# Sliding-window heads of a hybrid attention block: the softmax division moved to ScalarE, the low words of q placed by DMA, and the small softmax operations done once per head

## The chip, the core and the metric

One core of one Trainium2 chip runs the whole kernel as a single launch. The time is device microseconds (us) of that core, from the launch's start to its end; lower is better. The kernel before takes 830.82 us, the median of three runs (830.65 to 831.07).

## The reference

The block normalises x (512 tokens, 2048 channels), multiplies it by one wide input matrix, runs two groups of attention heads, gates each group with SiLU, multiplies by an output matrix, adds x and normalises again. The change lies in the second group alone: sixteen heads of 64 channels, two key/value heads, a window of 128 tokens and a learned sink per head.

```python
def _masked_softmax(s, mask, sink=None):
    s = jnp.where(mask, s.astype(jnp.float32), NEG_INF)
    m = jnp.maximum(jnp.max(s, axis=-1, keepdims=True), sink)
    e = jnp.where(mask, jnp.exp(s - m), 0.0)
    denom = jnp.sum(e, axis=-1, keepdims=True) + jnp.exp(sink - m)
    return e / jnp.maximum(denom, TINY)
...
qb = _rope(_heads(qb, N_HEADS_B, HEAD_DIM_B)).reshape(B, S, N_KV_B, GROUP_B, HEAD_DIM_B)
o_b = _banded_attention(qb, _rope(kb), vb, WIN_B, sink=sinks)   # blocks of 128 queries x 256 keys
y_b = o_b.reshape(B, S, WIDTH_B) * jax.nn.silu(zb)
```

## The kernel before

All products run on TensorE in single-precision "words": a float32 operand is split into a high word (rounded to the format that TensorE takes at full rate) and a low word (the rest), and a product is three matmuls, high by high, high by low, low by high (the helper `mm3`, L112 to L115). So each operand needs a copy that makes the high word (ScalarE, e.g. L89) and a subtraction that makes the low word (VectorE, e.g. L90).

The program is written as a sequence, and a planner puts it in order: it works through the program with an estimate of each instruction's time and gives every engine one fixed order, so work that stands later in the program fills the gaps of earlier work. Buffers come from tagged pools: a tile takes one of the `bufs` buffers of its tag and holds it until its last reader is done. A pool that is opened after another one was closed lies in the memory that the closed one leaves.

The stages: the first projections and the compressed keys (up to about 180 us); the eight heads of the first group, functions `pair` and `attn_a` (to about 471 us); the second group (to about 690 us), which the change touches; the output projection and the last normalisation.

The second group handles two heads at a time, in eight rounds i = 0 to 7 ("pair i" below). The loop at L880 to L896 does for each: `softmax_b(i)`; the projection of the next pair's q, `proj(wz[17+i])`, and its evacuation `qb_evac`; the gate projection `proj(wz[24+i])` with its evacuation `z_evac`; and `attn_b(i)`. Ahead of the loop stand the projection of the keys (L876), that of q for pair 0 (`wz[16]`, L877), and `build_k`, `build_v`, which make the words of keys and values.

- `proj` (L398) sums 48 matmuls of 512 columns into one bank of the accumulator memory, a tile with tag `pj`. That tag has two buffers, so a third projection can start only when one of the two before has been read out.
- `q_rope` (L463) reads the bank with three VectorE operations (L118, L119, L120) into `t1` and `t2`, which GpSimd adds (L468). `t1` and `t2` have one buffer each, and `z_evac` (L455) takes the `t2` buffer too for its `zr` (L458).
- `qb_evac` (L785) makes two operands of 128 rows from `t1`. ScalarE copies `t1` into both (L795). Then, for each of the two heads and each half of the channels, VectorE overwrites 32 rows with the low words of the 32 rows beside them (L799, four per pair). A matmul against the stacked keys so sums high and low words at once.
- `softmax_b` (L803) works in two parts of two query blocks each. In a part: the scores on TensorE (L820, L821), one VectorE operation per block and head that scales, masks and takes the row minimum (L824), the minimum with the sink (L827), the sink's exponent (L828, L829), the exponentials with their row sums on ScalarE (L834), the addition and the reciprocal (L835, L836), and the division as a multiplication by the reciprocal on VectorE (L841). The score blocks `ttb` have six buffers, the scores' banks `spb` two.
- `attn_b` (L844) transposes the blocks on TensorE (L855), splits them (L508, L509), multiplies by the values (L861, L862, L867) and evacuates (L871, L872, L489).

The pool `wb`, which holds `vbf`, `kd`, the keys' words, `ttb` and other tiles of this group, is opened at L751, after the pools of the first group were closed (L743, L746). The pool `wk` with `t1`, `t2` and the q operands is older and lasts through both groups. Once the last gate projection is done, the memory of x is closed (L889) and `yh`, `yl`, the words of the attention's output, are made there (L909, L910) for the output projection (accumulators `oa`).

Of the kernel before, what the change touches and what calls it, by code (L numbers as in the profile page):

```python
# [10 lines left out]
F32 = mybir.dt.float32  # L11
F32R = mybir.dt.float32r
AF = mybir.ActivationFunctionType
ALU = mybir.AluOpType
# [3 lines left out]
P = 128  # L18
S = 512
D = 2048  # L20
KT = D // P
NQ = S // P
# [4 lines left out]
SCALE_B = 64 ** -0.5  # L27
# [7 lines left out]
def hybrid_block(ctx, tc, xT, xtm, w0, w1s, w2s, wz, wq, wkb, wo0, wos, cw1, cw2, cpos, rope, tabs, sinks, gT, fg, out):  # L35
    nc = tc.nc
    pe, act, dve, pool = nc.tensor, nc.scalar, nc.vector, nc.gpsimd

    def sb(name, bufs=1, side=None):
        return tc.tile_pool(name=name, bufs=bufs, side=side)  # L40
# [8 lines left out]
    bmask = tab[:, 512 + NQ * CMP:768 + NQ * CMP]  # L49
# [413 lines left out]
    def q_rope(ps, cos, sin, t1=None):  # L463
        if t1 is None:
            t1 = wk.tile([P, S], F32, name="t1", tag="t1", bufs=1)
        t2 = wk.tile([P, S], F32, name="t2", tag="t2", bufs=1)
        rope_mul(t1, t2, ps, cos, sin)
        pool.tensor_tensor(out=t1, in0=t1, in1=t2, op=ALU.add)  # L468
        return t1
# [33 lines left out]
    wk = wks.enter_context(sb("wk", bufs=2))  # L503
# [102 lines left out]
    for m in range(8):  # L606
        j, r = m // 4, m % 4
# [142 lines left out]
    pssb = psb.enter_context(tc.tile_pool(name="pssB", bufs=2, space=PSUM, side="right"))  # L750
    wb = wbs.enter_context(sb("wb"))  # L751
# [33 lines left out]
    def qb_evac(ps, i):  # L785
        t1 = q_rope(ps, cosB, sinB)
        if i % 2:
            both = wk.tile([P, 2, S], F32R, name="qs", tag="raw3", bufs=1)
            where = [both[:, v, :] for v in range(2)]
        else:  # L790
            where = [wk.tile([P, S], F32R, name="qs", tag=f"q{w}", bufs=1) for w in "hl"]
        q2 = []
        for v in range(2):
            qs = where[v]
            act.activation(qs, t1, AF.Copy)  # L795
            for half in range(2):
                r = half * 64 + v * 32
                d = half * 64 + 32 - v * 32
                dve.tensor_tensor(out=qs[d:d + 32], in0=t1[r:r + 32], in1=qs[r:r + 32].bitcast(F32), op=ALU.subtract)  # L799
            q2.append(qs)  # L800
        return q2

    def softmax_b(i, q2):  # L803
        g = i // 4
        tts = []
        skb = sk[:, 0, 2 * i:2 * i + 2].unsqueeze(1).to_broadcast([P, 2, 2])
        nskb = sk[:, 1, 2 * i:2 * i + 2].unsqueeze(1).to_broadcast([P, 2, 2])
        for part in range(2):
            mn = wk.tile([P, 2, 2], F32, name="mnb", tag="mnb")
            dn = wk.tile([P, 2, 2], F32, name="dnb", tag="dnb")  # L810
            ex = wk.tile([P, 2, 2], F32, name="exb", tag="exb")
            for e in range(2):
                qt = 2 * part + e
                tt = wb.tile([P, 2, 256], F32, name="ttb", tag="ttb", bufs=6)
                tts.append(tt)
                ko = max(qt - 1, 0) * P
                qs = slice(qt * P, (qt + 1) * P)
                sp = pssb.tile([P, 2, 256], F32, name="spb", tag="spb")
                for v in range(2):
                    pe.matmul(sp[:, v, :], q2[v][:, qs], KBH[:, g, ko:ko + 256], start=v == 0, stop=False)  # L820
                    pe.matmul(sp[:, v, :], q2[v][:, qs], KBL[:, g, ko:ko + 256], start=False, stop=v == 1)  # L821
                n = 256 if qt else 128
                for v in range(2):
                    dve.tensor_tensor_reduce(out=tt[:, v, 0:n], in0=sp[:, v, 0:n], in1=bmask[:, 256 - n:256],  # L824
                                             scale=-SCALE_B, scalar=1e38, op0=ALU.add, op1=ALU.min,
                                             accum_out=mn[:, e, v:v + 1])
            dve.tensor_tensor(out=mn, in0=mn, in1=nskb, op=ALU.min)  # L827
            dve.tensor_tensor(out=ex, in0=mn, in1=skb, op=ALU.add)  # L828
            act.activation(ex, ex, AF.Exp)  # L829
            for e in range(2):  # L830
                n = 256 if part or e else 128
                for v in range(2):
                    tv = tts[2 * part + e][:, v, 0:n]
                    act.activation(tv, tv, AF.Exp, bias=mn[:, e, v:v + 1], scale=-1.0, accum_out=dn[:, e, v:v + 1])  # L834
            dve.tensor_tensor(out=dn, in0=dn, in1=ex, op=ALU.add)  # L835
            dve.reciprocal(dn, dn)  # L836
            for e in range(2):
                n = 256 if part or e else 128
                for v in range(2):
                    tv = tts[2 * part + e][:, v, 0:n]  # L840
                    dve.tensor_scalar(tv, tv, dn[:, e, v:v + 1], None, op0=ALU.mult)  # L841
        return tts

    def attn_b(i, tts, st):  # L844
# [164 lines left out]
    for t in range(NQ):  # L1009
        v = xs0[t // 2][:, t % 2, :]  # L1010
# [308 lines left out]
```

## Time and profile before

| | us |
|---|---|
| median of three runs | 830.82 |
| the profiled execution, device time | 829.19 |
| its span, first to last instruction | 827.4 |
| TensorE busy | 811.5 (98%) |
| VectorE busy | 662.1 (80%) |
| ScalarE busy | 485.6 (59%) |
| GpSimd busy | 89.3 (11%) |

The profile is of one execution. Its engines are PE (TensorE), PEld (TensorE's weight loads, beside PE), DVE (VectorE), ACT (ScalarE), POOL (GpSimd) and SP (the queue that issues most DMAs). L12 is line 12 of the kernel. A group's row gives engine, operation, output and inputs, shape and type, count, busy time and mean, and the idle time of its engine just before it with what ended that. Rows of a timeline begin with start and length in us. Rows of windows give start and end, then the window's length, then busy time and count of each engine, the granted clock of TensorE as a share of full speed, the DMA engines' busy share and GB/s. Times inside the profile count from the start of the span.

### The profile page before, as it was taken

The page shows a single profiled execution, that of the slowest core. Times are in us where ns is not written, and L with a number is a line of the kernel's source. Part 1 is how long each engine was busy: PE and PEld are TensorE (multiplying, and loading weights), DVE is VectorE, ACT ScalarE, POOL GpSimd, SP SyncE. Part 2 cuts the span into 40 slices and gives each one's busy share as a digit, 9 for nine tenths or more (in the row PEclk, how much of TensorE's full clock was granted, in tenths as well). Part 3 has the DMA queues.
Part 4 walks back from the last instruction along what each step waited for, and adds up shares of the span by engine and source line. Part 5 has one row for each costly group of instructions (what it writes and reads, how often), then busy time and mean ns, then how long its engine had stood idle before and what let it go on. Part 6 is the DMA issues. An engine that isn't in the chain of part 4 may idle for free.

```text
span 827.4 us, 14161 instructions
## 1 busy us (share of the span) xinstructions
PE 811.5 (98%) x5278; PEld 735.6 (89%) x5278; DVE 662.1 (80%) x1311; ACT 485.6 (59%) x1026; POOL 89.3 (11%) x69
## 2 busy tenths in 40 slices
PE   9999999999999999999999999999999999999996
PEld 7788898999999999999888888888888788999996
DVE  6869786966799898999766688877677798877895
ACT  6734456564676786787665365645444647554555
POOL 3600002011001001101011121011011000110000
PEclk9999999999999999999999999999999999999998
DMA  9665885898330222522733321222222226797845
GB/s 324 194 206 166 281 290 200 265 371 284 103 111 22 99 77 92 166 90 89 251 107 102 99 92 56 74 80 74 77 76 77 77 62 241 235 251 198 244 96 203
DMA packets 52117, 128.30 MB, mean 155 GB/s; under 512 B 4945, under 2 KB 17233, under 8 KB 52049
## 3 DMA queue, kind: packets, MB, share of 16 engines
q1 hardware_dynamic: 50032, 120.59, 43.3%
q0 software_dynamic: 1728, 6.29, 4.3%
q8 instruction: 41, 0.67, 0.3%
q10 hardware_dynamic: 288, 0.52, 0.2%
q14 instruction: 28, 0.22, 0.1%
HBM read 110.31 MB, written 17.07 MB: 154 GB/s over the span
## 4 chain that ended last, share of the span: by engine, by line
PE 84%; DVE 6%; DMA 5%; issue 2%; ACT 2%; SPq 0%; DVEq 0%; ACTq 0%; POOLq 0%
PE pj L115 16%; PE pj L113 15%; PE pj L114 15%; PE bank L115 4%; PE bank L113 4%; PE oa L114 4%; PE oa L113 4%; PE oa L115 3%; PE sp L539 3%; PE bank L114 3%; PE tp L855 2%; DMA rw<-wos 1%; PE tp L577 1%; DMA xr<-xT 1%; DMA raw<-cw 1%
## 5 line engine op out<-in xcount | busy, mean ns | idle before, releaser
L115 PE MATMUL pj<-xh,wlo 128*128 128x512 f32 (+1 forms) x560 | 196.0, 350 | 2.0 <-DVE wlo L617 1.5
L113 PE MATMUL pj<-xh,whi 128*128 128x512 f32 (+1 forms) x560 | 196.2, 350 | 0.8 <-DVE t L665 0.8
L114 PE MATMUL pj<-xl,whi 128*128 128x512 f32 (+1 forms) x560 | 195.4, 349 | 0.0
L90 DVE TENSOR_TENSOR wlo<-raw,whi 128x1024 fp32r<-128x1024 f32 (+2 forms) x102 | 115.3, 1135 | 37.5 <-ACT whi L89 36.6
L89 ACT ACTIVATE whi<-raw 128x1024 fp32r<-128x1024 f32 (+1 forms) x101 | 95.2, 944 | 80.6 <-PE pj L114 24.0
L115 PEld LDWEIGHTS pj<-xh,wlo 128*128 128x128 f32 x560 | 105.3, 188 | 16.3 <-DVE wlo L617 2.2
L113 PEld LDWEIGHTS pj<-xh,whi 128*128 128x128 f32 x560 | 105.4, 188 | 14.2 <-DVE t L665 1.2
L114 PEld LDWEIGHTS pj<-xl,whi 128*128 128x128 f32 x560 | 105.3, 188 | 13.4 <-issue 0.7
L617 DVE TENSOR_TENSOR wlo<-raw,whi 128x1024 fp32r<-128x1024 f32 x49 | 61.6, 1260 | 10.3 <-ACT whi L616 9.9
L616 ACT ACTIVATE whi<-raw 128x1024 fp32r<-128x1024 f32 x49 | 51.7, 1056 | 24.7 <-PE pj L114 12.7
L113 PE MATMUL oa<-whi,yh 128*128 128x256 f32 (+1 forms) x168 | 50.1, 299 | 0.6 <-ACT yh L909 0.6
L114 PE MATMUL oa<-wlo,yh 128*128 128x256 f32 (+1 forms) x168 | 50.4, 300 | 0.2 <-DVE wlo L1147 0.2
L115 PE MATMUL oa<-whi,yl 128*128 128x256 f32 (+1 forms) x168 | 49.7, 299 | 0.0
L834 ACT ACTIVATE ttb<-ttb,mnb 128x256 f32<-128x256 f32 (+1 forms) x64 | 30.1, 471 | 26.0 <-DVE mnb L827 25.5
L509 DVE TENSOR_TENSOR pl<-tp,ph 128x512 fp32r<-128x512 f32 x56 | 37.6, 683 | 6.6 <-ACT ph L508 6.6
L508 ACT ACTIVATE ph<-tp 128x512 fp32r<-128x512 f32 x56 | 32.3, 592 | 17.9 <-PE tp L577 11.2
L114 PE MATMUL bank<-wlo,xh 128*128 128x256 f32 (+1 forms) x128 | 40.2, 316 | 0.0
L115 PE MATMUL bank<-whi,xl 128*128 128x256 f32 (+1 forms) x128 | 39.9, 314 | 0.0
L468 POOL TENSOR_TENSOR t<-t,t 128x512 f32<-128x512 f32 x9 | 19.3, 2147 | 176.4 <-DVE t L120 176.4
L113 PE MATMUL bank<-xh,whi 128*128 128x512 f32 x96 | 37.0, 396 | 1.1 <-ACT whi L89 0.7
L113 PE MATMUL bank<-whi,xh 128*128 128x256 f32 (+1 forms) x128 | 36.7, 318 | 1.3 <-ACT whi L89 1.3
L114 PE MATMUL bank<-xl,whi 128*128 128x512 f32 x96 | 37.0, 391 | 0.0
(356 smaller groups left out, 2202.2 us busy)
## 6 DMA issues: line engine op xcount, KB each, us to landing
raw<-wz SPq DMA_DIRECT2D x36, 512.0 KB, 3.6
raw<-wq SPq DMA_DIRECT2D x28, 512.0 KB, 3.7
raw<-cw SPq DMA_DIRECT2D x16, 512.0 KB, 5.0
raw<-wos SPq DMA_DIRECT2D x12, 512.0 KB, 5.0
rw<-wos SPq DMA_DIRECT2D x10, 512.0 KB, 5.5
xr<-xT SPq DMA_DIRECT2D x16, 256.0 KB, 5.0
raw<-w SPq DMA_DIRECT2D x8, 512.0 KB, 4.2
fd<-ft SPq DMA_DIRECT2D x4, 1024.0 KB, 5.9
```

Of the source, the lines that this page charges most:

```text
L89: last["hi"] = act.activation(hi[:, :width], rw[:, :width], AF.Copy).ins
L90: last["lo"] = dve.tensor_tensor(out=lo[:, :width], in0=rw[:, :width], in1=hi[:, :width].bitcast(F32), op=ALU.subtract).ins
L113: pe.matmul(ps, ah, bh, start=first, stop=False, skip_group_check=go_on)
L114: pe.matmul(ps, ah, bl, start=False, stop=False, skip_group_check=go_on)
L115: recent["mm"] = pe.matmul(ps, al, bh, start=False, stop=last, skip_group_check=go_on).ins
L468: pool.tensor_tensor(out=t1, in0=t1, in1=t2, op=ALU.add)
L508: act.activation(ph, tp, AF.Copy)
L509: dve.tensor_tensor(out=pl, in0=tp, in1=ph.bitcast(F32), op=ALU.subtract)
L539: pe.matmul(sp[:, a:b], qq[:, qs], kk[0][:, ko:ko + b - a], start=pi == 0, stop=pi == 2)
L616: act.activation(hi, src, AF.Copy)
L617: last["lo"] = dve.tensor_tensor(out=lo, in0=src, in1=hi.bitcast(F32), op=ALU.subtract).ins
L834: act.activation(tv, tv, AF.Exp, bias=mn[:, e, v:v + 1], scale=-1.0, accum_out=dn[:, e, v:v + 1])
```

## The change

In `qb_evac`, one subtraction over all 128 rows makes a tile `low` (new, in the pool `wb`, one buffer), and four DMAs on the SP queue place its quarters, 32 rows of 2 KB each, into the two q operands. In `softmax_b` the two parts become one: the small tiles hold all four query blocks, and L827, L828, L829, L835 and L836 are issued once per pair in place of twice. The division is a ScalarE copy with a scale per row in place of a VectorE multiplication. The score blocks still have six buffers. No matmul is added or taken away.

```diff
+        low = wb.tile([P, S], F32R, name="low", tag="low")
+        for qs in where:
             act.activation(qs, t1, AF.Copy)
+        dve.tensor_tensor(out=low, in0=t1, in1=where[0].bitcast(F32), op=ALU.subtract)
+        for v, qs in enumerate(where):
             for half in range(2):
                 r = half * 64 + v * 32
                 d = half * 64 + 32 - v * 32
-                dve.tensor_tensor(out=qs[d:d + 32], in0=t1[r:r + 32], in1=qs[r:r + 32].bitcast(F32), op=ALU.subtract)
+                nc.sync.dma_start(qs[d:d + 32].bitcast(F32), low[r:r + 32].bitcast(F32))
...
-        for part in range(2):
-            mn = wk.tile([P, 2, 2], F32, name="mnb", tag="mnb")
+        mn = wk.tile([P, NQ, 2], F32, name="mnb", tag="mnb")
+        for qt in range(NQ):
...
+        dve.tensor_tensor(out=mn, in0=mn, in1=nskb, op=ALU.min)
+        dve.tensor_tensor(out=ex, in0=mn, in1=skb, op=ALU.add)
+        act.activation(ex, ex, AF.Exp)
+        for qt in range(NQ):
+            for v in range(2):
+                tv = tts[qt][:, v, 0:256 if qt else 128]
+                act.activation(tv, tv, AF.Exp, bias=mn[:, qt, v:v + 1], scale=-1.0, accum_out=dn[:, qt, v:v + 1])
+        dve.tensor_tensor(out=dn, in0=dn, in1=ex, op=ALU.add)
+        dve.reciprocal(dn, dn)
...
-                    dve.tensor_scalar(tv, tv, dn[:, e, v:v + 1], None, op0=ALU.mult)
+                act.activation(tv, tv, AF.Copy, scale=dn[:, qt, v:v + 1])
```

More of the change, by code (lines that the diff above doesn't have):

```diff
@@ L791, in qb_evac @@
             where = [wk.tile([P, S], F32R, name="qs", tag=f"q{w}", bufs=1) for w in "hl"]
-        q2 = []
-        for v in range(2):
-            qs = where[v]
+        low = wb.tile([P, S], F32R, name="low", tag="low")
+        for qs in where:
             act.activation(qs, t1, AF.Copy)
+        dve.tensor_tensor(out=low, in0=t1, in1=where[0].bitcast(F32), op=ALU.subtract)
+        for v, qs in enumerate(where):
             for half in range(2):
@@ L798, in qb_evac @@
                 d = half * 64 + 32 - v * 32
-                dve.tensor_tensor(out=qs[d:d + 32], in0=t1[r:r + 32], in1=qs[r:r + 32].bitcast(F32), op=ALU.subtract)
-            q2.append(qs)
-        return q2
+                nc.sync.dma_start(qs[d:d + 32].bitcast(F32), low[r:r + 32].bitcast(F32))
+        return where
     def softmax_b(i, q2):
@@ L805, in softmax_b @@
         tts = []
-        skb = sk[:, 0, 2 * i:2 * i + 2].unsqueeze(1).to_broadcast([P, 2, 2])
-        nskb = sk[:, 1, 2 * i:2 * i + 2].unsqueeze(1).to_broadcast([P, 2, 2])
-        for part in range(2):
-            mn = wk.tile([P, 2, 2], F32, name="mnb", tag="mnb")
[L810 to L841, printed above, removed]
@@ new lines, in softmax_b @@
+        skb = sk[:, 0, 2 * i:2 * i + 2].unsqueeze(1).to_broadcast([P, NQ, 2])
+        nskb = sk[:, 1, 2 * i:2 * i + 2].unsqueeze(1).to_broadcast([P, NQ, 2])
+        mn = wk.tile([P, NQ, 2], F32, name="mnb", tag="mnb")
+        dn = wk.tile([P, NQ, 2], F32, name="dnb", tag="dnb")
+        ex = wk.tile([P, NQ, 2], F32, name="exb", tag="exb")
+        for qt in range(NQ):
+            tt = wb.tile([P, 2, 256], F32, name="ttb", tag="ttb", bufs=6)
+            n = 256 if qt else 128
+            tts.append(tt)
+            ko = max(qt - 1, 0) * P
+            qs = slice(qt * P, (qt + 1) * P)
+            sp = pssb.tile([P, 2, 256], F32, name="spb", tag="spb")
+            for v in range(2):
+                pe.matmul(sp[:, v, :], q2[v][:, qs], KBH[:, g, ko:ko + 256], start=v == 0, stop=False)
+                pe.matmul(sp[:, v, :], q2[v][:, qs], KBL[:, g, ko:ko + 256], start=False, stop=v == 1)
+            for v in range(2):
+                dve.tensor_tensor_reduce(out=tt[:, v, 0:n], in0=sp[:, v, 0:n], in1=bmask[:, 256 - n:256],
+                                         scale=-SCALE_B, scalar=1e38, op0=ALU.add, op1=ALU.min,
+                                         accum_out=mn[:, qt, v:v + 1])
@@ new lines, in softmax_b @@
+        dve.tensor_tensor(out=mn, in0=mn, in1=nskb, op=ALU.min)
+        dve.tensor_tensor(out=ex, in0=mn, in1=skb, op=ALU.add)
+        act.activation(ex, ex, AF.Exp)
+        for qt in range(NQ):
+            for v in range(2):
+                tv = tts[qt][:, v, 0:256 if qt else 128]
+                act.activation(tv, tv, AF.Exp, bias=mn[:, qt, v:v + 1], scale=-1.0, accum_out=dn[:, qt, v:v + 1])
+        dve.tensor_tensor(out=dn, in0=dn, in1=ex, op=ALU.add)
+        dve.reciprocal(dn, dn)
+        for qt in range(NQ):
+            for v in range(2):
+                tv = tts[qt][:, v, 0:256 if qt else 128]
+                act.activation(tv, tv, AF.Copy, scale=dn[:, qt, v:v + 1])
```

## The prediction

> **What bounds the kernel now.** I read the windows first, then TensorE's waits, then the timelines around the two ends of the second group. Windows (start and end, length, then busy us of PE, PEld, DVE, ACT, POOL, the granted clock, DMA share, GB/s):
>
> ```profile
> 478.00:655.00 177.00, 177.00 (x927) 148.67 (x926) 139.03 (x374) 92.17 (x232) 14.98 (x8) 1.00 0.24 76
> 657.00:700.00 43.00, 43.00 (x195) 34.83 (x196) 39.91 (x86) 26.93 (x55) 0.00 (x0) 1.00 0.39 127
> 700.00:819.00 119.00, 118.76 (x1024) 117.66 (x1023) 99.22 (x128) 64.12 (x98) 10.64 (x12) 1.00 0.74 213
> ```
>
> All waits of TensorE between 430 and 710 us (what waited, on whom, us in total, times, longest):
>
> ```profile
> PE oa L113 <- ACT yh L909: 0.6, 1, 0.6
> ```
>
> The reader is to see that TensorE has work in hand through the whole second group, 177.00 of 177.00 us, and goes on so to 819 us. VectorE is busy for 139 of those 177 us, but TensorE never waits for it. The only wait in the group is 0.6 us at its end. Busy could still be slow, so I looked at the pace: the 512-column matmuls start 0.23 us apart (468.64 and 468.87 in a fence below) at a granted clock of 1.00. The change takes away no matmul. So it can gain at most about 0.6 us here, whatever it does for VectorE, and it can lose wherever TensorE runs out of work. The question is which tile comes later than before.
>
> **The change part by part.** The sum is made against the profiled execution, 829.19 us (its span of 827.4 and 1.8 around it). That is 1.6 under the median of the three runs, 830.82; I add the difference found to the median.
>
> *Amounts.* Groups by shape, 440 to 700 us (the ScalarE rows from 330 to 700):
>
> ```profile
> L799 DVE TENSOR_TENSOR qs<-t,qs 32x512 fp32r<-32x512 f32 x32 | 21.8, 683 | 1.6 <-ACT qs L795 0.7
> L841 DVE TENSOR_SCALAR ttb<-ttb,dnb 128x256 f32<-128x256 f32 x48 | 14.4, 357 | 0.2
> L841 DVE TENSOR_SCALAR ttb<-ttb,dnb 128x128 f32<-128x128 f32 x16 | 3.8, 283 | 0.2
> L910 DVE TENSOR_TENSOR yl<-yp,yh 128x512 fp32r<-128x512 f32 x16 | 10.4, 677 | 0.2 <-ACT yh L909 0.2
> L567 ACT ACTIVATE tt<-tt,dn 128x256 f32<-128x256 f32 x8 | 3.6, 499 | 0.0
> L567 ACT ACTIVATE tt<-tt,dn 128x128 f32<-128x128 f32 x8 | 2.7, 392 | 0.0
> L834 ACT ACTIVATE ttb<-ttb,mnb 128x256 f32<-128x256 f32 x48 | 23.8, 497 | 9.5 <-DVE mnb L827 9.0
> ```
>
> VectorE loses the 32 quarter subtractions (21.8 us) and the divisions (14.4 + 3.8 = 18.2), gains eight subtractions of 128x512 at 0.68 as in L910 (5.4), and does half of its small operations: some 35 us less, and more with the small ones. ScalarE gains 48 x 0.50 + 16 x 0.39 = 30.2 us, as L567 shows for the same scaling in the first group. In the 177 us window ScalarE is busy for 92, so it has room on average. Both amounts are off TensorE's path, and I cost them at nothing in the middle of the group. The cover is the product work that TensorE has in hand.
>
> *Middle of the group.* Rounds repeat every 27.9 us. Of one round (engine timelines):
>
> ```profile
> 593.68 0.15 DVE L827 TENSOR_TENSOR mnb<-mnb,sk 128x4 f32<-128x4 f32 x1
> 596.49 1.14 DVE L841 TENSOR_SCALAR ttb<-ttb,dnb 128x256 f32<-128x256 f32 x4
> 604.47 1.15 ACT L795 ACTIVATE qs<-t 128x512 fp32r<-128x512 f32 x2 [3.38 <-POOL t L468]
> 605.14 2.79 DVE L799 TENSOR_TENSOR qs<-t,qs 32x512 fp32r<-32x512 f32 x4
> 610.65 1.03 PE L855 MATMUL tp<-ident,ttb 128*128 128x128 f32 x8
> 611.44 0.36 PE L820 MATMUL spb<-KBH,qs 128*128 128x256 f32 x1
> ```
>
> The score blocks are divided by 597.6 and transposed at 610.65: 13 us to spare. Done at once per pair, the last minimum still comes near 593.7. Then follow eight exponentials (6 x 0.50 + 2 x 0.39 = 3.8), the sums and reciprocal (0.4) and eight divisions (3.8), which ends near 602 and leaves 8. The q operands are ready at 607.9 and used at 611.44, so 3.5 to spare. In their place: first copy 605.1, `low` 605.8, four issues of 0.33 (as that of `vbf` below), and a landing. No row shows a 64 KB transfer between two tiles. The nearest are (KB each, median us from issue to landing):
>
> ```profile
> yd<-st SPq DMA_DIRECT2D x8, 256.0 KB, 2.4
> sk<-sinks SPq DMA_DIRECT2D x1, 8.0 KB, 4.5
> raw<-wz SPq DMA_DIRECT2D x36, 512.0 KB, 3.6
> ```
>
> That puts the last quarter between 609.2 and 611.3, still ahead of 611.44. I take 0, by the row that also leaves a tile of this core; the other end, behind a weight load (another 3.6), is 3.5 us in a round, and I keep half a microsecond a round, 3.5 for seven, in the range. The issues stand in SP's queue ahead of weight loads, which wait for `low` with them; these loads wait for a free buffer anyway (the queue's rows put 132 us on that, quoted below), so a microsecond costs nothing.
>
> *Start of the group.* Here I expect the loss. `low` lives in the pool `wb`; the quarter subtractions of before wrote only into `wk`. When does `wb`'s memory come free? SP's waits from 440 to 660 us, then timelines:
>
> ```profile
> SPq L85 <- DVE wlo L90: 132.4, 23, 8.6
> SPq L758 <- PE op L600: 0.2, 1, 0.2
> ...
> 446.22 2.77 DVE L799 TENSOR_TENSOR qs<-t,qs 32x512 fp32r<-32x512 f32 x4
> 449.02 0.17 DVE L556 TENSOR_SCALAR dn<-dn 128x6 f32<-128x6 f32 x1
> 454.62 0.69 DVE L118 TENSOR_TENSOR t<-pj,cosA 128x512 f32<-128x512 f32 x1 [3.41 <-PE pj L115]
> 468.84 0.69 DVE L458 TENSOR_TENSOR zr<-pj,rstdb 128x512 f32<-128x512 f32 x1 [2.56 <-PE pj L115]
> 471.49 0.69 DVE L489 SCALAR_TENSOR_TENSOR st<-op,st 128x512 f32<-128x512 f32 x1
> 471.48 0.33 SPq L758 DMA_DIRECT2D vbf<-vbd x1
> 472.10 1.70 DVE L776 COPY kd<-kb 32x512 f32<-32x512 f32 x4
> ...
> 468.64 0.39 PE L113 MATMUL pj<-xh,whi 128*128 128x512 f32 x1
> 468.87 0.39 PE L114 MATMUL pj<-xl,whi 128*128 128x512 f32 x1
> 470.84 0.61 PE L600 MATMUL op<-pd,VF 128*128 128x128 f32 x4
> ```
>
> `vbf`, the first tile of `wb`, waits for L600, the last matmul of the first group, though that matmul has nothing to do with `vbf`; so the pool as a whole seems to come free when L600 ends, at 470.84 + 0.61 = 471.45. Before, pair 0's low words were written at 446 to 449, which released `t1`, and pair 1's rotation (L118) read its bank at 454.62. With the change `low` of pair 0 waits for L600, so `t1` stays taken and pair 1's rotation waits. Its bank of `pj` stays taken too. The other bank gets the gate product of pair 0 (read out at 468.84), whose `zr` wants the buffer of `t2`, and the waiting rotation holds that if its L119 goes ahead. Then the next product has no bank. Before, it began at 468.64 (the next starts 0.23 later), and six of its matmuls stand ahead of L600's end. Without them L600 is done near 471.45 - 6 x 0.23 = 470.1, and TensorE is out of work.
>
> What it waits for then: `low` (0.68), `kd` (1.70, earlier in the program), L118 (0.69), 0.1 of signalling, 3.2 in all. VectorE's freed 2.8 us at 446 let L556 start about 0.6 earlier (it was queued behind L799), and L600 with it. I take 3.2 - 0.6 = **2.6 us**. Ends: 0 if the gate's evacuation frees a bank in time; 5.2 if L489 (0.69) and both L119 and L120 (1.4) come in the same stretch and nothing is gained earlier. Only a late operand of pair 0 could follow, but its keys' words are ready no earlier than near 474 either.
>
> *End of the group.* The last pair has no next q product to hide behind. Timelines:
>
> ```profile
> 647.33 0.60 PE L855 MATMUL tp<-ident,ttb 128*128 128x128 f32 x4
> 648.52 1.05 ACT L89 ACTIVATE whi<-raw 128x1024 fp32r<-128x1024 f32 x1
> 655.24 1.06 ACT L89 ACTIVATE whi<-raw 128x1024 fp32r<-128x1024 f32 x1
> 655.27 1.03 PE L855 MATMUL tp<-ident,ttb 128*128 128x128 f32 x8
> 656.21 4.26 ACT L909 ACTIVATE yh<-yp 128x512 fp32r<-128x512 f32 x8
> ```
>
> The third and fourth score blocks need buffers that the pair before gives back with its last transposes (647.33). Before, only the second part's four exponentials came after that; VectorE divided, TensorE transposed at 655.27, and ScalarE was free for `yh`, for which TensorE waits. After, ScalarE has eight exponentials from 649.6, behind the weight copy (3.8, to 653.4), sums (0.4), eight divisions (3.8, or 3.2 overlapped as neighbours) to about 657.2, and a weight copy of 1.06 that may stand before or between. `yh` moves from 656.2 to between 656.2 (if it is put ahead of the divisions) and 659.6; the transposes move into the gap. I take **1.2 us**, from 656.2 to the end of the divisions plus a signal, with bounds -0.6 (the wait of today gone) and 3.4. Behind it, VectorE is busy for 39.9 of 43 us and keeps its order, and I add nothing.
>
> Sum: 2.6 + 1.2 = 3.8 us; 829.2 becomes 833.0, and on the median 830.8 + 3.8 = **834.6 us**.
>
> **Rivals.** *The gate's evacuation goes first.* If the planner gives `t2`'s buffer to `zr` at 468.84, a bank is free at 469.5, before TensorE runs out at 470.1, and the start costs nothing. For it: VectorE idles 2.56 us there. Against it: L119 could run from 454.6 and takes `t2` earlier. What decides is which of the two writes that buffer first. With the end at 1.2 or less the time is 830.3 to 832.0, 831.4 by the middle: not slower by the bound below. The same time results if `low` lies in memory that is free before L600; the wait of `vbf` speaks against it. 34%.
>
> *The hold is longer and the clock drops.* At the end of the run the clock follows TensorE's idleness (last matmul ends at 819.8):
>
> ```profile
> 819.55 0.28 PE L115 MATMUL oa<-whi,ql 128*128 128x256 f32 x1
> ...
> 822.00:824.00 2.00, 0.00 (x0) 0.00 (x0) 0.60 (x1) 0.78 (x2) 0.00 (x0) 0.77 0.61 226
> 824.00:828.00 4.00, 0.00 (x0) 0.00 (x0) 0.00 (x0) 0.00 (x0) 0.00 (x0) 0.50 0.40 149
> ```
>
> A mean of 0.77 between 1.00 and 0.50 puts the drop at 823.1, 3.3 us after the last matmul. My 2.6 stays below that, the upper end 5.2 does not. How long half speed would last no row shows; if as long as the drop took, 3.3 us at half pace lose 1.7. Then 5.2 + 1.7 + 1.2 = 8.1, 838.9 us; without the drop, but with 3.5 for late quarters, 3.8 + 3.5 = 7.3, 838.1. 14%. The Trainium skill, TensorE: Matmul & The Clock Gate, section HAM oscillation, states that idle gaps over about 3.4 us bring the half clock back; by its window an estimate of the loss is 1.7 us, and the trace agrees on the drop with 3.3 us.
>
> *Relief of VectorE pays.* Gone wait at 656 and an order with fewer gaps between 700 and 819 (0.24 idle there): 0.6 + 0.24, 830.0 us, inside the bound. A gain beyond it would need matmuls closer than 0.23 us, which nothing here does. 6% for a gain by a way that I don't see, at about 828.5.
>
> **How the numbers follow.** Forecast 46% (832.6 to 836.5), first rival 34%, second 14%, relief 6%. A difference of 0.2%, 1.7 us, is about what a measurement of this kernel can tell from no change. Faster 0.06; same 0.34; slower 0.46 + 0.14 = 0.60. The range leaves out the gain and the part of the long hold above 838.5: 829.9 to 838.5.
>
> **What would show it.** Right at the start: `low` of pair 0 begins just after L600, the second L118 of the group moves from 454.6 to beyond 470, and TensorE shows a wait on VectorE of 2 to 4 us near 470. Wrong: `low` at about 446, or L458 still at 468.8 with no wait. Right at the end: `yh` near 657.5 behind L841's copies, and TensorE waits 1 us or more there. In the middle: no wait of TensorE on SP's transfers; waits at L820 would mean that the quarters land late. The forecast as a whole is wrong if TensorE's idle time is the same as before.

## The result, and the profile after

The changed kernel takes 842.52 us (median of 4 runs, 841.38 to 843.52) against 830.95 us for the kernel before (4 runs, 830.65 to 831.37): the ratio is 1.0134, 95% interval 1.0115 to 1.0152. It is some 11.6 us slower; the forecast was 3.8 slower, and 842.52 lies above the range. The profiled execution took 841.38 us, its span is 839.6 (before: 829.19 and 827.4). Lines of the changed kernel's page are a few lower than before: the q copies are L794, `low` L795, its DMAs L800, the scores L819 and L820, the division L837, the transposes L851, `yh` L905.

The windows after, with the same columns as those of before in the prediction:

```profile
478.00:655.00 177.00, 177.00 (x924) 148.29 (x923) 101.75 (x252) 105.72 (x261) 13.62 (x7) 1.00 0.27 82
657.00:700.00 43.00, 41.91 (x197) 33.52 (x196) 34.37 (x71) 27.30 (x60) 0.00 (x0) 1.00 0.29 86
700.00:819.00 119.00, 115.06 (x950) 111.91 (x950) 99.10 (x133) 63.69 (x100) 10.63 (x12) 1.00 0.74 208
```

TensorE's waits over the whole of the changed kernel, the four that touch the second group or what follows it:

```profile
PE spb L819 <- DMA qs<-low: 7.4, 1, 7.4
PE oa L114 <- DVE wlo L910: 3.5, 3, 1.7
...
PE oa L113 <- ACT yh L905: 1.1, 1, 1.1
...
PE oa L114 <- DVE wlo L1143: 0.5, 1, 0.5
```

The reader is to see that VectorE's busy time in the middle falls from 139 to 102 us and that TensorE still has work for 177.00 of 177.00: the relief is there and buys nothing. The loss stands at the seams, 7.4 us at the start of the group and 3.5 in the output projection.

**The start.** TensorE, then VectorE, then SP's queue:

```profile
467.59 0.60 PE L600 MATMUL op<-pd,VF 128*128 128x128 f32 x4
475.63 0.77 PE L819 MATMUL spb<-KBH,qs 128*128 128x256 f32 x2 [7.43 <-DMA qs<-low]
476.19 0.63 PE L113 MATMUL pj<-xh,whi 128*128 128x512 f32 x1
...
478.33 0.58 PE L115 MATMUL pj<-xh,wlo 128*128 128x512 f32 x1
478.74 0.40 PE L113 MATMUL pj<-xh,whi 128*128 128x512 f32 x1
```

```profile
467.82 1.23 DVE L90 TENSOR_TENSOR wlo<-raw,whi 128x1024 fp32r<-128x1024 f32 x1 [4.11 <-ACT whi L89]
469.08 0.69 DVE L489 SCALAR_TENSOR_TENSOR st<-op,st 128x512 f32<-128x512 f32 x1
469.69 0.68 DVE L795 TENSOR_TENSOR low<-t,qs 128x512 fp32r<-128x512 f32 x1
470.29 1.70 DVE L776 COPY kd<-kb 32x512 f32<-32x512 f32 x4
472.02 0.69 DVE L118 TENSOR_TENSOR t<-pj,cosA 128x512 f32<-128x512 f32 x1
...
473.43 0.68 DVE L120 TENSOR_TENSOR t<-pj,sinA 64x512 f32<-64x512 f32 x1
475.59 0.69 DVE L458 TENSOR_TENSOR zr<-pj,rstdb 128x512 f32<-128x512 f32 x1 [1.48 <-POOL t L468]
```

```profile
468.23 0.33 SPq L758 DMA_DIRECT2D vbf<-vbd x1
...
470.39 2.76 SPq L800 DMA_DIRECT2D qs<-low x4
```

`low` of pair 0 comes after L600, and pair 1's rotation (L118) moved from 454.62 to 472.02. L600 ends at 468.19. Until the wait's end at 475.63 stand, in order: a weight split and L489 (1.50), `low` (0.60), `kd` (1.73), L118 to L120 (2.09, to 474.11), and 1.52 until the last quarter lands. The four DMAs are issued from 470.39 on, beside `kd` and the rotation, so only their last 1.52 us add to the wait. The scores of pair 0, which read the quarters, stand in TensorE's order ahead of the third product. The first matmuls then start 0.43 us apart instead of 0.23. Windows around it, same columns:

```profile
470.00:472.00 2.00, 0.00 (x0) 0.00 (x0) 1.95 (x5) 0.73 (x2) 0.36 (x1) 0.97 0.80 178
472.00:474.00 2.00, 0.00 (x0) 0.00 (x0) 1.95 (x3) 0.63 (x1) 2.00 (x2) 0.50 0.88 314
...
476.00:478.00 2.00, 2.00 (x7) 1.61 (x7) 0.68 (x2) 1.96 (x5) 0.00 (x0) 0.50 0.39 131
478.00:480.00 2.00, 2.00 (x9) 1.62 (x8) 0.99 (x2) 1.13 (x3) 0.79 (x1) 0.82 0.14 33
```

A mean of 0.97 puts the clock's drop near 471.9, 3.7 us after the last matmul; full speed is back by 478.74. The two score matmuls took 0.56 instead of 0.24 to the next start, and the six starts from 476.19 to 478.74 took 2.55 instead of 1.38: half speed cost 1.5 us. With the wait, 8.9 us.

**The end.** ScalarE, TensorE, VectorE and SP after the last pair's scores:

```profile
661.24 0.49 ACT L831 ACTIVATE ttb<-ttb,mnb 128x256 f32<-128x256 f32 x1
...
662.68 3.22 ACT L905 ACTIVATE yh<-yp 128x512 fp32r<-128x512 f32 x6
...
666.43 2.70 ACT L905 ACTIVATE yh<-yp 128x512 fp32r<-128x512 f32 x5
669.03 3.08 ACT L837 ACTIVATE ttb<-ttb,dnb 128x128 f32<-128x128 f32 x8
...
663.35 0.50 PE L113 MATMUL oa<-whi,yh 128*128 128x512 f32 x1 [1.09 <-ACT yh L905]
...
701.78 0.69 DVE L489 SCALAR_TENSOR_TENSOR yp<-ob,st 128x512 f32<-128x512 f32 x1
702.55 0.89 SPq L1004 DMA_DIRECT2D xs<-xtm x2
```

The same two kinds of event in the kernel before, with its first output matmul:

```profile
656.87 0.50 PE L113 MATMUL oa<-whi,yh 128*128 128x512 f32 x1 [0.56 <-ACT yh L909]
...
691.41 0.69 DVE L489 SCALAR_TENSOR_TENSOR yp<-ob,st 128x512 f32<-128x512 f32 x1
692.19 0.89 SPq L1008 DMA_DIRECT2D xs<-xtm x2
```

The planner put eleven `yh` copies ahead of the last pair's eight divisions. The last pair is therefore finished (L489) 38.4 us after the first output matmul, where it was 34.5. In both kernels the first load into the last stage's new pools (`xs`) starts within 0.1 us of that L489's end: the program opens these pools after it has closed `wb` and `wk`. So the loads into them (`xs`, then `rw` and `ch`) come 3.9 us later against the work that needs them. TensorE waits 3.5 us for low words of weights (L910), in three places, and not all of them are for these loads:

```profile
715.59 1.21 DVE L910 TENSOR_TENSOR wlo<-raw,whi 128x1024 fp32r<-128x1024 f32 x1
...
716.86 0.39 PE L114 MATMUL oa<-wlo,ph 128*128 128x256 f32 x1 [1.68 <-DVE wlo L910]
...
728.71 0.39 PE L114 MATMUL oa<-wlo,yh 128*128 128x256 f32 x1 [0.79 <-DVE wlo L910]
```

The first, 1.7 us, is for words of a `raw`, a buffer from before, whose load was issued by 696.8, ahead of that L489. VectorE has had no gap since 702.38, and the planner put this split behind four additions (L1007): this wait comes from VectorE's queue and not from a late load. Only the other two, 1.8 us together, are for words of `ch`, which is loaded behind L489.

Put together from these rows, against the profile of before: the first q evacuation was 1.8 us earlier (439.13 against 440.97; the change is not in that stretch), from there to the first output matmul it takes 224.22 against 215.90, 8.3 more, and from there to the span's end 176.25 against 170.53, 5.7 more: -1.8 + 8.3 + 5.7 = 12.2, the difference of the spans. TensorE's waits tell the same without the opening: all in the list of waits come to 8.1 us before and 18.9 after, 10.8 more, and with 1.5 at half speed that is 12.3. So the -1.8 is work that the planner placed elsewhere, not a gain.

### The profile page after: what moved, and what is told of

The parts are those of the page before. It is cut to its first block, busy times and chain, and to the rows that moved or that the text cites. A ratio compares the mean times of both kernels' runs of the same rounds, so it can differ in the third digit from the quotient of the medians.

```text
span 839.6 us, 14182 instructions
## 1 busy us (share of the span) xinstructions
PE 813.3 (97%) x5278; PEld 736.5 (88%) x5278; DVE 624.4 (74%) x1191; ACT 507.0 (60%) x1082; POOL 88.2 (11%) x69
## 4 chain that ended last, share of the span: by engine, by line
PE 79%; DVE 7%; DMA 7%; ACT 3%; issue 3%; POOL 1%; SPq 0%; DVEq 0%; ACTq 0%; POOLq 0%
PE pj L115 15%; PE pj L113 15%; PE pj L114 15%; PE bank L115 4%; PE bank L113 4%; PE bank L114 3%; PE sp L539 3%; PE oa L114 3%; PE oa L113 3%; PE oa L115 3%; DMA rw<-wos 2%; PE tp L851 1%; DMA ch<-wos 1%; PE tp L577 1%; DMA xr<-xT 1%
## 5 line engine op out<-in xcount | busy, mean ns | idle before, releaser
L115 PE MATMUL bank<-whi,xl 128*128 128x256 f32 (+1 forms) x128 | 39.9, 314 | 0.0
L822 DVE CUSTOM_DVE_ANT_0 ttb<-spb,tab 128x256 f32<-128x256 f32 (+1 forms) x64 | 22.1, 386 | 21.6 <-PE spb L820 17.9
L665 DVE TENSOR_TENSOR raw<-raw 128x1024 f32<-128x1024 f32 x28 | 36.2, 1291 | 0.2
```

Of the source, the lines that this page charges most:

```text
L115: recent["mm"] = pe.matmul(ps, al, bh, start=False, stop=last, skip_group_check=go_on).ins
L665: return dve.tensor_tensor(out=out, in0=a, in1=b, op=op).ins
```

## The experiments

Four theories. A: the start's loss comes from the memory given to `low`. A1, a closer form: what costs is that `t1` is held, which stops pair 1's rotation. C: the end's loss comes from the divisions on ScalarE. D: it comes from the softmax done once per pair. The results in one table; each ratio is to the kernel before on the same chip, whose median was 830.67 for the first four, 829.11 for the next four and 831.48 for the last four. "kb1" is the unused second half of kb1's tile, which lies in the old pool `wk`.

| kernel | low words | softmax | division | us | ratio, 95% interval |
|---|---|---|---|---|---|
| low_old | DMA, kb1 | once | ScalarE | 834.52 | 1.0050, 1.0030 to 1.0069 |
| t1_two | DMA, wb | once | ScalarE | 836.87 | 1.0073, 1.0048 to 1.0097 |
| direct | VectorE | once | ScalarE | 836.09 | 1.0063, 1.0046 to 1.0081 |
| div_dve | DMA, wb | once | VectorE | 842.98 | 1.0146, 1.0110 to 1.0182 |
| once_pair | VectorE | once | VectorE | 831.92 | 1.0033, 1.0019 to 1.0048 |
| div_act | VectorE | halves | ScalarE | 828.80 | 0.9989, 0.9974 to 1.0004 |
| low_dma | DMA, kb1 | halves | VectorE | 832.51 | 1.0026, 1.0010 to 1.0042 |
| low_dma_act | DMA, kb1 | halves | ScalarE | 829.55 | 1.0005, 0.9989 to 1.0022 |
| low_wb | DMA, wb | halves | VectorE | 844.18 | 1.0148, 1.0122 to 1.0175 |
| wb_direct0 | DMA, wb; pair 0 VectorE | halves | VectorE | 838.74 | 1.0093, 1.0070 to 1.0117 |
| last_two | DMA, kb1 | last pair in halves | ScalarE | 830.87 | 0.9996, 0.9978 to 1.0014 |
| last_once | DMA, kb1 | only last pair once | ScalarE | 835.19 | 1.0047, 1.0032 to 1.0062 |

### The start: low_old, t1_two, low_wb, wb_direct0

**low_old**, on the changed kernel:

```diff
-    kb1 = wk.tile([P, 2, S], F32, name="kb1", tag="xr", bufs=1)[:, 0, :]
+    kbx = wk.tile([P, 2, S], F32, name="kb1", tag="xr", bufs=1)
+    kb1 = kbx[:, 0, :]
...
-        low = wb.tile([P, S], F32R, name="low", tag="low")
+        low = kbx[:, 1, :].bitcast(F32R)
```

> The changed kernel, but `low` lies in an old buffer: the unused second half of the tile of `kb1`, in the pool `wk`, in place of the pool `wb`. Theory A (the memory of `wb` comes free late, with L600, and holds `t1` and a bank): pair 0's `low` runs near 444 us, TensorE's wait of 7.4 us near 470 and the half clock behind it (about 1.4 us) go, and 842.5 becomes 833.7; the loss at the end of the group stays. Rival B (the transfers themselves are slow or stand behind other loads, wherever `low` lies): TensorE still waits for the quarters near 470, and the time stays above 839.

834.52 us, 8.0 less than the changed kernel's median. VectorE, then TensorE's waits from 430 to 830 us:

```profile
445.33 0.69 DVE L795 TENSOR_TENSOR kb<-t,qs 128x512 fp32r<-128x512 f32 x1
...
454.00 0.69 DVE L118 TENSOR_TENSOR t<-pj,cosA 128x512 f32<-128x512 f32 x1 [0.59 <-PE pj L115]
```

```profile
PE oa L114 <- DVE wlo L911: 3.1, 3, 1.6
PE oa L113 <- ACT yh L906: 1.9, 1, 1.9
PE oa L114 <- DVE wlo L1144: 0.3, 1, 0.3
```

`low` (under the name `kb`, that of kb1's tile) is made at 445, the rotation stands at 454 again and no wait is left at the start. The waits at the end stay. So the loss has two parts, and theory A holds for the first.

**t1_two**, on the changed kernel: `low` stays in `wb`, but pair 1 rotates into another `t1`.

```diff
-        t1 = q_rope(ps, cosB, sinB)
+        t1 = q_rope(ps, cosB, sinB, kbx[:, 1, :] if i == 1 else None)
```

> The changed kernel with `low` in `wb` as it is, but pair 1's rotation writes into a buffer of its own (the unused half of the tile of `kb1`) and not into `t1`. Theory A1 (the loss is that `t1` holds pair 1's bank): pair 1's L118 runs near 453 us, the third q product starts near 467, TensorE has work, and the time is 834 to 836. Theory A2 (what counts is that the scores of pair 0, put ahead of that product, wait for the quarters): a wait of 5 us or more for the quarters stays, and the time is above 838.

836.87 us, a little over the 834 to 836 expected; its last stage also ran at the slower of two paces (below). VectorE:

```profile
454.28 0.69 DVE L118 TENSOR_TENSOR kb<-pj,cosA 128x512 f32<-128x512 f32 x1 [0.59 <-PE pj L115]
...
471.73 0.68 DVE L795 TENSOR_TENSOR low<-t,qs 128x512 fp32r<-128x512 f32 x1
```

`low` still comes after L600, at 471.73, and nobody minds: TensorE shows no wait at the start. The late `low` costs only through the `t1` that it holds, as A1 has it. With the bank free, the third product runs through L600's end here and stands ahead of pair 0's scores (479.41), so it covers the first quarters too.

**low_wb** is the kernel before with the change's lines of `qb_evac` alone (`low` in `wb`, the four DMAs); **wb_direct0** is low_wb with this for pair 0:

```diff
+        if i == 0:
+            for v, qs in enumerate(where):
+                act.activation(qs, t1, AF.Copy)
+                for half in range(2):
...
+                    dve.tensor_tensor(out=qs[d:d + 32], in0=t1[r:r + 32], in1=qs[r:r + 32].bitcast(F32), op=ALU.subtract)
+            low = wb.tile([P, S], F32R, name="low", tag="low")
+            dve.tensor_copy(low, t1)
+            return where
```

> The kernel before with one part of the change alone, in the memory that the change gives it: low words by DMA, low in pool wb; softmax in two halves, division on VectorE. The theory of the held t1 (the memory of wb is free when the first group's last matmul ends; t1 and the two banks are held until then): 7 to 9 us slower than low_dma, which differs from it in the memory alone, so 8.5 to 11.5 us slower than before; a wait of TensorE between 7 and 8 us at the start. If the start's loss needs the other parts too (the order that once per pair and ScalarE's division bring): less than 5 us slower than before.

> As low_wb, but pair 0's quarters are written by VectorE from t1, ahead of time, and a copy of t1 into pair 0's low words (which nothing reads) holds t1 and the memory just as before. It leaves out nothing of the result. Theory that the quarters' DMAs add to the held bank: TensorE's wait at the start falls from about 7.4 us to 5 to 6, and the time is 1.5 to 3 us below low_wb. Rival, that the bank alone sets it: the wait stays at 7 or more and the time within 0.5 us of low_wb.

TensorE in low_wb:

```profile
477.68 0.77 PE L820 MATMUL spb<-KBH,qs 128*128 128x256 f32 x2 [7.86 <-DMA qs<-low]
...
482.51 0.59 PE L114 MATMUL pj<-xl,whi 128*128 128x512 f32 x1
482.94 0.40 PE L115 MATMUL pj<-xh,wlo 128*128 128x512 f32 x1
```

and in wb_direct0:

```profile
474.43 0.50 PE L830 MATMUL spb<-KBH,qs 128*128 128x256 f32 x2 [4.25 <-ACT KBH L777]
475.89 0.79 PE L113 MATMUL pj<-xh,whi 128*128 128x512 f32 x1 [0.96 <-DVE t L120]
```

low_wb needs none of the change's other parts for the start's wait. It is 12.7 us slower than before, a little over the 8.5 to 11.5 expected: half speed lasted 5.2 us here (477.68 to about 482.9) and not 3.1, and TensorE waits 2.0 for weights (L914) in the last stage. Without pair 0's DMAs the wait falls from 7.86 to 4.25 + 0.96 = 5.2, as the theory of the added quarters had it, and ends with the rotation itself (L120). The time falls by 5.4, more than the 1.5 to 3 expected; the profile of low_wb also ran its last stage at another pace (below). The 2.0 us for weights stay in wb_direct0.

### The end: direct, div_dve, once_pair, div_act, low_dma, low_dma_act

**direct** is the changed kernel with the quarter subtractions of before in place of `low` and its DMAs. **div_dve** is the changed kernel with

```diff
-                act.activation(tv, tv, AF.Copy, scale=dn[:, qt, v:v + 1])
+                dve.tensor_scalar(tv, tv, dn[:, qt, v:v + 1], None, op0=ALU.mult)
```

> The changed kernel with the low words of q made as before, by four VectorE subtractions straight into the operands; division on ScalarE and once per pair stay. Theory A: the loss at the start is gone and the loss at the end stays, 833 to 835. Rival: the DMAs also cause the loss at the end (their queue delays the weight loads), and the time is within 0.2% of 830.9.

> The changed kernel with the division back on VectorE; low words by DMA and once per pair stay. Theory C (the last pair's divisions on ScalarE stand behind the words of y, so the last pair ends late and the memory for the last stage's loads comes late): the waits of 3.5 us for L910 after 720 us and half of the wait near 663 go, and 842.5 becomes 837 to 838. Rival D (once per pair is what makes the last pair late): the time stays within 1 us of 842.5.

direct takes 1.0063 times the time of before, within the interval of low_old, but that doesn't show the end's loss in it: 836.09 us is above the 833 to 835 expected, its TensorE waits come to 8.6 us against 8.1 before, none of them for weights in the last stage, and that stage runs at the slower of two paces, some 4 us (below). div_dve shows no gain by giving the division back (1.0146, the changed kernel 1.0134). The waits for low words of weights (3.5 us) are gone there, but its last pair's transposes, which the planner now put ahead of the `yh` words, wait 1.9 us for VectorE's divisions, the last stage waits 1.0 for high words of a weight, and TensorE runs longer at half speed: 10.2 us at the start of the group and 3.4 at its end (last section). So div_dve alone doesn't decide on theory C; the next four do.

The next four isolate the parts. **once_pair** is the change's `softmax_b` alone, with the division on VectorE as in div_dve. **div_act** is the kernel before with one line:

```diff
-                    dve.tensor_scalar(tv, tv, dn[:, e, v:v + 1], None, op0=ALU.mult)
+                    act.activation(tv, tv, AF.Copy, scale=dn[:, e, v:v + 1])
```

**low_dma** is the kernel before with the change's `qb_evac`, `low` in kb1 as in low_old; **low_dma_act** is low_dma with div_act's line.

> The kernel before with one part of the change alone: the small softmax operations once per pair and not in two halves. Low words and division stay as they were, on VectorE. What is left to explain after the memory of the low words has gone back is 834.52 - 830.67 = 3.9 us. Theory D (once per pair: all eight divisions wait for the last of eight exponentials, so the last pair's transposes come late): 834 to 835. Theory C (the division on ScalarE delays the last pair): within 0.5 of before, about 831. If both parts are needed together: below 832 here and in the run with ScalarE's division alone.

> The kernel before with the division by the sums on ScalarE alone; two halves and low words as before. Theory C: 834 to 835. Theory D: 830.5 to 831.5, and the last pair's transposes wait no longer than before. The rival that VectorE's relief pays: below 829.5.

> The kernel before with one part of the change alone, in memory that is free early: low words made once by a full-width subtraction and placed by four DMAs, the low words in the unused half of kb1's tile; softmax in two halves, division on VectorE. Theories C and D both: 830.5 to 831.5, since TensorE has work all through the group and waits for no quarter, and no wait at the start. A rival, that the DMAs themselves cost (the quarters land 1.9 to 4.9 us after their issue, and late scores keep ScalarE and the last pair back): 832 to 835. VectorE's relief pays: below 829.5.

> The whole change but once per pair: low words by DMA in the unused half of kb1's tile, division on ScalarE, small softmax operations in two halves as before. Theory D: about 831 (830.5 to 832), as once per pair is all that costs at the end. Theory C: 834 to 835, as low_old. VectorE's relief pays once nothing delays the end: below 829.5.

once_pair alone loses 0.33%; its TensorE waits at the end of the group (below) and from 657.4 to 660.9 runs at half speed, which costs 1.7 us; in the last stage it waits 1.0 for high words of a weight:

```profile
656.54 0.69 PE L848 MATMUL tp<-ident,ttb 128*128 128x128 f32 x2 [1.92 <-DVE ttb L834]
```

The loss of 2.8 us is below the 3.9 of theory D, and 831.92 and div_act's 828.80 meet what was expected if both parts are needed together (both below 832). div_act alone is not told apart from before: the division on ScalarE costs nothing by itself, against theory C. low_dma_act, which has all of the change but once per pair (and its `low` in the old memory), is level with before, where low_old, once per pair, loses 0.50%: theory D. So once per pair is needed for the loss, and enough for most of it; that ScalarE's division adds the rest (3.9 against 2.8) is not ruled out. A miss: low_dma was to be level too, and loses 0.26%, as its rival (the DMAs cost) had it; but low_dma_act has the same DMAs. Its profile shows 3.5 us of waits for weights in the last stage; 2.0 of them are again for words of a `raw`, whose split the planner put behind the last of the four additions (706.80), where before has it ahead of the last two. So this wait comes with the planner's order and needs no late last pair; no run changed that order alone. The other 1.5 us stay open, with the last pair finished when before has it (L489 at 691.80). An unchanged kernel can show some of it (before_2, below).

### Which pair: last_two, last_once

Both are low_dma_act with a softmax whose number of blocks per part depends on the pair:

```diff
-        for part in range(2):
+        ne = 2 if i == 7 else NQ
+        for part in range(NQ // ne):
```

for last_two, and `NQ if i == 7 else 2` for last_once.

> The whole change, with low in the unused half of kb1's tile (no loss at the start), and the last pair's softmax in two halves as before; the other seven pairs once. low_old, which differs in the last pair alone, was 3.9 us slower than before, and low_dma_act, all eight pairs in two halves, 0.4. Theory that once per pair costs in the last pair alone, where TensorE has nothing else to do: within 1 us of before. Rival, that all eight pairs cost (scores, transposes and the order around them): 3 to 5 us slower.

> The reverse of last_two: only the last pair's softmax once, the other seven in two halves; low in the unused half of kb1's tile, division on ScalarE. Theory that the last pair alone costs: 3 to 5 us slower than before, with a gap of 2 us or more in TensorE at the end of the group and late weights in the last stage. Rival, all eight pairs: within 1 us of before.

With the last pair in halves and seven pairs once, the time is that of before (0.9996). With the last pair alone once, it is 1.0047. So the other seven cost nothing, as TensorE's product work covers them, and the last pair makes the loss: last_two and low_old differ in that pair alone and ran their last stage at the same pace. In last_once the planner put the eight divisions ahead of `yh`. ScalarE, then TensorE:

```profile
652.85 3.07 ACT L842 ACTIVATE ttb<-ttb,dnb 128x128 f32<-128x128 f32 x8
...
653.98 1.13 PE L856 MATMUL tp<-ident,ttb 128*128 128x128 f32 x4 [0.36 <-ACT ttb L842]
655.57 0.73 PE L856 MATMUL tp<-ident,ttb 128*128 128x128 f32 x3 [0.47 <-ACT ttb L842]
657.44 0.80 PE L113 MATMUL oa<-whi,yh 128*128 128x512 f32 x1 [1.14 <-ACT yh L911]
```

The eight transposes follow the divisions' pace: from the first (653.31) to the first output matmul it takes 4.1 us, where before takes 1.6 (655.27 to 656.87). `yh` comes behind both, and no weight is waited for in the last stage, where late weights were expected. In low_old and the changed kernel the same work stands the other way round, and weights are waited for. The way the loss arises so changes with the planner's order, which is read from the traces and not tested by itself. Of the 3.7 us by which last_once is slower, the half clock from 657.3 to 660.7 accounts for 1.7; its TensorE waits come to 8.0 us in all, as before. How much is the pace of its last stage, 172 matmuls in 20 us as in direct, is not told apart.

### The pace of the last stage: before_2, before_3, direct_2, low_wb_2

No edit: three kernels profiled again, in one run each.

> The kernel before, unchanged, profiled once more. In the profiles so far the last stage runs at one of two paces at a granted clock of 1.00: 178 to 179 matmuls in 20 us (740 to 760) in ten kernels, this one among them, and 172 in four (t1_two, direct, low_wb, last_once), which makes some 4 us over the stage. Theory that the pace belongs to the execution: 172 can show here too, and the profiled time is then about 4 us longer. Rival, that the pace belongs to the kernel: 178 to 179 in each profile of this kernel.

> The kernel of direct, unchanged, profiled once more. The pace belongs to the execution: 178 to 179 matmuls between 740 and 760 us can show here, where the first profile showed 172, and the time is then about 4 us shorter for the same gaps. It belongs to the kernel: 172 again.

> The kernel of low_wb, unchanged, profiled once more, with 172 in its first profile. The pace belongs to the execution: 178 to 179 can show here, with a time near 841. It belongs to the kernel: 172 again, with a time near 845.

> The kernel before, unchanged, profiled a third time, with the same two theories as before_2: 172 matmuls between 740 and 760 us in one of the profiles would show that the pace belongs to the execution.

Times of 832.42, 828.95 (before), 834.78 (direct) and 843.01 (low_wb). The window from 740 to 760 us of low_wb:

```profile
740.00:760.00 20.00, 20.00 (x172) 20.00 (x172) 14.21 (x16) 10.72 (x16) 1.73 (x2) 1.00 0.97 275
```

and of low_wb_2, the same kernel:

```profile
740.00:760.00 20.00, 20.00 (x179) 20.00 (x178) 14.50 (x17) 11.27 (x16) 1.74 (x2) 1.00 0.91 258
```

One kernel shows both counts, so the pace belongs to the execution at least in part. (The two times differ by 1.2 us only, as low_wb_2 has a second stretch at half speed, 720.1 to 723.5, which costs 1.7.) But direct had 172 both times and before 178 to 179 three times, so a kernel seems to lean to one; what decides is open. before_2 was 3.5 us longer than before_3 at the same pace: it waits 2.2 us for weights in the last stage, which the other profiles of before hardly show. They are words of `ch`, whose loads were issued as in the first profile of before (694.24 against 694.11); the second was ready 3 us later (716.53 against 713.46).

No version here beats the kernel before beyond its interval; div_act (0.9989) and last_two (0.9996) are level with it.

## Why the prediction was wrong in size

- **TensorE is the bound in the middle, no gain from VectorE's relief: right.** 177.00 of 177.00 us with work; div_act, which moves all divisions off VectorE, is level with before.
- **The quarters hide in the middle: right.** They land 2.0 us (median) after their issue, and no wait of TensorE on them shows after 476. The first pair's are the exception.
- **Start, 2.6 us: the mechanism was right, the size failed.** `wb`'s memory comes free with L600, `t1` is held, the rotation and the bank wait: low_old and t1_two show the memory and `t1`. The working summed `low`, `kd`, L118 and a signal, 3.2, and credited 0.6. Seen: 7.4 of wait and 1.5 of half speed. The weight split and L489 ahead of `low` cost 1.5 and L119 and L120 1.4; the text had the last three as its upper end of 5.2. Then the quarters, 1.5, which the step excluded ("Only a late operand of pair 0 could follow, but its keys' words are ready no earlier than near 474 either"): the scores stand ahead of the product, and without the DMAs they could start 4.25 us after L600 (wb_direct0) where they start 7.86 after it with them (low_wb). The credit of 0.6 did not come: corrected by the 1.8 us of the first q evacuation, L600 ended at 470.03, just where the six missing matmuls put it (470.07).
- **The clock.** The second rival, with 14%, had the drop at 3.3 us after the last matmul and 1.7 us lost; seen were 3.7 and 1.5. It took late quarters and the drop as alternatives, and they came together. The Trainium skill, TensorE: Matmul & The Clock Gate, section What's actually happening, has the clock halve after an idle window of about 3.4 us and return after a busy one. 3.7 here is near the first, but div_dve shows 2.6 and low_wb_2 4.6 after the last matmul: no one length counted from there fits (last section).
- **The first rival** (gate's evacuation first) did not come: `zr` (L458) ran at 475.59, behind the `t2` that L119 took.
- **End, 1.2 us: the step "Behind it, VectorE is busy for 39.9 of 43 us and keeps its order, and I add nothing" failed.** The wait for `yh` itself grew by 0.5 in the changed kernel and by 1.3 in low_old (0.6 to 1.9), near the forecast. What was left out lies behind it. VectorE did not keep its order against TensorE: with the divisions behind eleven `yh` words its L489 is 3.9 us late against the output projection. TensorE waits 1.7 us for a split that stands in VectorE's queue behind it, and 1.8 us for words of `ch`, whose loads start at that L489. That the last pair done once makes the loss is shown by time (last_two); that it does so through these waits is read from the traces.

Start 8.9, waits for weights 3.5 and the wait for `yh` 0.5 come to 12.9, near the 12.2 between the profiles; the smaller waits of the rest of the kernel are 0.6 less, which leaves 12.3.

## What to carry to other kernels

A new tile brings the wait of its memory with it: look in the trace when that pool's first tile is written, list what its producer holds until then, and follow each held buffer to TensorE with all that is queued ahead, not just the one instruction. Steps that a busy engine hides in every round are bare in the last one, so change the last round by itself, and follow its end to the memory that it releases. Where a new gap may bring the half clock, add its stretch as a chance and not by the gap's length alone: waits of 2 us, in one piece or in three close together, brought it in some executions of this case and not in others.

## What the hardware showed that was not expected

The time from the first matmul after a gap to full speed differs: 3.1 us in the changed kernel (475.63 to 478.74) and 5.2 in low_wb (477.68 to about 482.9), both with matmuls back to back. The clock also fell where no gap was long. These two windows are of one kernel, with the same three waits at the end of the group (0.36, 0.47 and 1.14 us), first direct, then direct_2:

```profile
658.00:660.00 2.00, 1.84 (x8) 1.53 (x9) 2.00 (x4) 2.00 (x5) 0.00 (x0) 1.00 0.20 27
```

```profile
658.00:660.00 2.00, 2.00 (x7) 1.52 (x6) 2.00 (x5) 1.98 (x4) 0.00 (x0) 0.52 0.66 147
```

direct_2 is at half speed from 658.2 to 661.6, direct is not. last_once, with such waits, and once_pair and div_dve, each after one wait of 1.9, show it there too, and low_wb_2 after one wait of 2.0 us (720.1 to 723.5). Worked out from the windows' mean clocks, the half-speed stretches of these traces and of the changed kernel's start last 3.4, 6.8 or 10.2 us, whole multiples of 3.41, and two changes of one trace lie whole multiples of it apart (in low_wb_2 481.16 to 720.09, 70 times 3.413; in div_dve 482.63 to 666.95, 54 times). So in these traces the clock changes on a grid of 3.41 us, which lies elsewhere in each execution. The Trainium skill, TensorE: Matmul & The Clock Gate, section What's actually happening, describes a free-running window of about 3.4 us, so that the return depends on where in it the work starts; the grid agrees. A whole idle window is not needed here, though: the 3.4 us before the drop were idle for 1.4 in direct_2. How much is enough stays open.

The last stage's 256-column matmuls, each with its own weight load (PEld is busy for 20.00 of 20 us), run 172 or 178 to 179 in 20 us at a granted clock of 1.00, some 4 us over the stage. No engine or clock in the rows differs with it.
